# Both feature halves of a token tile projected in one block in every second attention step

## The chip, the cores and the metric

The kernel runs on one core of one Trainium2 chip. The metric is device time in microseconds (us) from the start to the end of the program. The engines are named as in the profile: PE is TensorE (matrix products; PEld are its weight loads), DVE is VectorE, ACT is ScalarE, POOL is GpSimd, and SP is SyncE, which here only issues DMAs. PE writes its results to PSUM, which has eight banks of 512 float32 per partition; DVE and ACT read them there, POOL and the DMAs cannot.

## The reference, cut to what matters

```python
def encoder_layer(x, w_in, rpb, w_fourier, b_fourier, g_pre, g_na, g_f, w_out, g_post):
    h = rms_norm(x, g_pre)
    q, k, v, z_a, u_f, z_f = jnp.split(h @ w_in, [...], axis=-1)     # 512 columns each
    y_a = neighbourhood_attention(q, k, v, rpb)   # 8 heads of 64, window 8 rows x 16 columns
    y_f = fourier_mix(u_f, w_fourier, b_fourier)  # fft2, then @ w_fourier + b_fourier
    mixed = jnp.concatenate([rms_norm(y_a, g_na) * jax.nn.silu(z_a),
                             rms_norm(y_f, g_f) * jax.nn.silu(z_f)], axis=-1)
    out = mixed @ w_out                           # (tokens, 1024) @ (1024, 1024)
    return x + rms_norm(out, g_post)
```

It is applied to a prompt of 256 tokens and to a sample of 2048 tokens (a grid of 32 rows by 64 columns), 2304 tokens together, in float32.

## The kernel before, in words

The kernel works in four stages: the input projections (up to about 554 us), the Fourier part (to about 611 us), a stage of 36 steps that computes the attention and beside it the Fourier half of the output projection (to about 850 us), and the attention half of the output projection with the last norm (to the end). The change lies in the third stage.

**A step.** The attention is cut into 36 groups, `G[0]` to `G[35]`: nine for each of four pairs of heads (`pr, i = divmod(k, 9)`). Group `i == 0` is the prompt (a block of 128 key columns), `i == 1, 2` are the top and bottom rows of the sample, and `i == 3` to `8` are its middle rows, the largest kind. Every group has two blocks of query columns (`b`), one with 32 and one with 24 key columns a row, and two heads (`h`), so four tiles of scores. The loop over `k` from 2 to 37 is a software pipeline. In step `k`

- `transp` turns the finished probabilities of group `k-2` on PE into four banks, `ptb[0]` to `ptb[3]`; ACT and DVE copy two banks each to the tile `pt`;
- `scores` forms the four score tiles of group `k` on PE. Three lie in the three banks of the ring `"a"`, the fourth (`b = 1, h = 1`) in the single bank of the ring `"c"`;
- `bias_max` (DVE, an instruction for each score tile and one that reads its accumulator) adds the bias and takes the row maximum; `exps` (ACT) takes the exponential; `soft` takes the reciprocal of the sums (DVE) and scales the probabilities (POOL, two instructions a block);
- `f_mm` multiplies a tile of 128 tokens of the Fourier half by one half (512 columns) of the output weights: twelve matmuls, since both factors are split in a high and a low part;
- `pv` multiplies the probabilities of group `k-2` by the values. Its result goes to the same single bank `"c"`, and is read there by DVE (`y`, times the gate) and by ACT (`sqa` or `ysq`, the squares).

**The projection beside it.** `ftiles[t]` is a tile of 128 tokens, 18 in all. `ys_load` fetches it, `ys_mul` (POOL) multiplies it by its gate, `ys_split` makes the high part `yh` (ACT) and the low part `yl` (DVE). Step `k` projects one feature half, `k % 2`, of tile `k // 2`. `f_evac` takes the result out of PSUM, scaled by the norm factor `invf`: the first half on DVE, the second on ACT, and a DMA stores the tile `ofs`. `f_norm` (in steps 4, 8, 10, 12) and `a_norm` (32, 34, 36) sum squares on PE and start the computation of norm factors, which `run_later` finishes. `YSQ` squares the last two blocks of the Fourier output in steps 2 to 7.

**What sets the order.** In this stage all five engines run their instructions in the order in which the program writes them; nothing reorders them. An instruction that waits holds up all that stands behind it on its engine. Semaphores between engines follow from the tiles: who reads a bank must have finished before PE writes it again.

The end of a step before, from `f_mm` on:

```python
            f_mm(k)
        ...
        run_later()
        ...
        if k % 2 and x < 18:
            ys_split(ftiles[x])
        ...
        if g:
            f_evac(k)
        pv(f)
```

Of the kernel before, what the change touches and what calls it, by code (L numbers as in the profile page):

```python
# [13 lines left out]
ALU = mybir.AluOpType  # L14
# [165 lines left out]
def build(tc, A, O):  # L180
# [976 lines left out]
    def scores(g):  # L1157
        nr = g["nr"]
        kk = KK[g["pr"]].rearrange("p (r c) -> p r c", c=64)
        if "w" in g:  # L1160
            sp = [ps.tile([128, 352], F32, tag="c", name="s", bufs=1), *ptb,
                  ps.tile([128, 352], F32, tag="a", name="s", bufs=3)]
        else:
            sp = [ps.tile([128, 352], F32, tag="c" if x == 3 else "a", name="s", bufs=1 if x == 3 else 3)
                  for x in range(4)]
        R = g["R"]
        for b, w in enumerate(g["kw"]):
            if R is None:
                seq = [(y, 0, 4, 0, KP0[2 * b + y]) for y in range(2)]
            else:  # L1170
                c0, r = KC0[2 * g["hc"] + b], 4 + HALF[R][0] - 4 * (R > 0)
                seq = [(0, r, 11, 0, c0), (1, r + 12, 3, 0, c0), (1, r + 4, 8, 3, c0)] if R else \
                    [(y, r + 24 * y, 8, 0, c0) for y in range(2)]
            for y, k, n, j, c0 in seq:
                for h in range(2):
                    hs = slice(64 * h, 64 * h + 64)
                    nc.tensor.matmul(sp[2 * b + h][64 * y:64 * y + 64, j * w:(j + n) * w],  # L1177
                                     g["q"][hs, 128 * b + 64 * y:128 * b + 64 * y + 64],
                                     kk[hs, k:k + n, c0:c0 + w], start=True, stop=True)
        g["s"] = sp  # L1180
        if "w" in g:
            return
        wide = [w == 32 and (g["R"] is not None or b) for b, w in enumerate(g["kw"])]
        g["w"] = [jp.tile([128, 2, 352 if x else 264], F32, tag="ww" if x else "wn", name="w", bufs=WB) for x in wide]
        g["m"] = [jp.tile([128, 8], F32, tag="m", name="m", bufs=4) for b in range(2)]
# [4 lines left out]
    def bias_max(g, b, h):  # L1190
        nr, w = g["nr"], g["kw"][b]
        n = nr * w
        if g["R"] is None:
            tv = rows(TB[g["pr"], 0][:, (2 * b + h) * n:(2 * b + h) * n + n], w)
        else:
            x0 = (g["R"] == 0) * 512 + h * nr * 80
            c0 = (0, 24, 24, 56)[2 * g["hc"] + b]
            tv = rows(TB[g["pr"], int(g["R"] > 0)][:, x0:x0 + nr * 80], 80)[:, :, c0:c0 + w]
        nc.vector.tensor_tensor_reduce(out=rows(g["w"][b][:, h, :n], w), in0=rows(g["s"][2 * b + h][:, :n], w), in1=tv,  # L1199
                               scale=1.0, scalar=3.0e38, op0=ALU.add, op1=ALU.min, accum_out=g["m"][b][:, h:h + 1])  # L1200
# [5 lines left out]
    def soft(g, b):  # L1206
        m = g["m"][b]
        nc.vector.reciprocal(m[:, 4:6], m[:, 2:4])  # L1208
        for h in range(2):
            w = g["w"][b][:, h, :g["nr"] * g["kw"][b]]  # L1210
            nc.gpsimd.tensor_scalar(w, w, m[:, 4 + h:5 + h], 1.0, ALU.mult, ALU.mult)  # L1211
# [175 lines left out]
    def ys_load(d):  # L1387
        t, half = d["t"], d["half"]
        ts = slice(t * 128, t * 128 + 128)
        d["raw"] = sm.tile([128, 4, 128], F32, tag="yr", name="yr", bufs=3)  # L1390
        nc.sync.dma_start(d["raw"], yD[half, :, :, ts].rearrange("c p t -> p c t"))
        if half:
            d["z"] = sm.tile([128, 4, 128], F32, tag="yz", name="yz", bufs=1)
            nc.sync.dma_start(d["z"], zD[0, :, ts].rearrange("(c p) t -> p c t", p=128))

    def ys_mul(d):
        if d["half"]:
            nc.gpsimd.tensor_tensor(out=d["raw"], in0=d["raw"], in1=d["z"], op=ALU.mult)
# [19 lines left out]
    def out_mm(d, n, js, p, w):  # L1418
        for j in js:
            c, x = divmod(j, 3)  # L1420
            nc.tensor.matmul(p, (d["l"] if x == 2 else d["h"])[:, c], w(n, int(x == 1), c), start=j == 0, stop=j == 11)  # L1421
# [6 lines left out]
        d["xt"] = gt([128, D], F32, "xt")  # L1428
        nc.sync.dma_start(d["xt"], A["xn"][d["t"] * 128:d["t"] * 128 + 128, :])

    def bank(k):
        return ptb[k if k < 2 else 2 + k % 2]

    def f_mm(k):
        d, n = ftiles[k // 2], k % 2
        d["p"] = bank(k)
        out_mm(d, n, range(12), d["p"], lambda n, x, c: wo1[n][c][:, x])

    def a_mm(d, n):
        x = n or d is atiles[0]  # L1440
# [1 line left out]
        d["p", n] = p  # L1442
        out_mm(d, n, range(12), p, lambda n, x, c: WO[x][:, c, n * 512:n * 512 + 512])

    def f_evac(k):
        d, n = ftiles[k // 2], k % 2
        t, p = d["t"], d.pop("p")
        if n == 0:
            d["o"] = gt([128, D], F32, "ofs")
        o = d["o"]  # L1450
        ns = slice(n * 512, n * 512 + 512)
        if n:
            nc.scalar.activation(o[:, ns], p, AF.Copy, scale=invf[:, t:t + 1])
            nc.sync.dma_start(oD[t * 128:t * 128 + 128, :], o)
        else:
            V.tensor_scalar(o[:, ns], p, invf[:, t:t + 1], None, ALU.mult)  # L1456
# [33 lines left out]
    def pv(g):  # L1490
# [35 lines left out]
        if R is None or hc:  # L1526
# [8 lines left out]

    NT = {4: range(2, 4), 8: range(4, 8), 10: range(8, 13), 12: range(13, 18)}

    YSQ = {2: [(Y2, 256, 512), (Y2, 512, 1024)], 3: [(Y, 256, 512), (Y2, 1024, 1664)], 4: [(Y2, 1664, 2304)],
           5: [(Y, 512, 1110)], 6: [(Y, 1110, 1708)], 7: [(Y, 1708, 2304)]}
    ftiles[0]["h"], ftiles[0]["l"] = y0h  # L1540
    y_parts(ftiles[1])
    ftiles[1]["raw"], ftiles[1]["z"] = y0[:, 0], y0[:, 1]
    nc.sync.dma_start(yD[1, 3, :, TP:], Y[:, TP:])
    f_mm(0)
    f_norm(range(2))
    ys_mul(ftiles[1])
    ptb += [ps.tile([128, 512], F32, tag="b", name="ptb", bufs=2) for x in range(2)]
    for x in range(2, 4):
        V.memset(ptb[x], 0.0)
    run_later()  # L1550
    f_evac(0)
    f_mm(1)
    ys_split(ftiles[1])
    f_evac(1)
    ys_load(ftiles[2])
    prep_v(G[2])
    prep(G[4])
# [1 line left out]
    for k in range(2, len(G) + 2):  # L1559
        pr, i = divmod(k, 9)  # L1560
        g, p, f = G[k] if k < len(G) else None, G[k - 1] if k <= len(G) else None, G[k - 2]
        if pr < 3:
            if i == 3:
                load_k(pr + 1)
            if i == 5:
                load_t(pr + 1, 0)
        if 0 < pr < 4 and i == 0:
            load_t(pr, 1)
        if k == 9:
            nc.sync.dma_start(gpb, pbc(A["gpost"]))  # L1570
        if k == 23:
            wp = pt.enter_context(tc.tile_pool(name="wp", bufs=1, side="right"))
            WO.extend(wp.tile([128, 4, D], F32R, name="w0%d" % x) for x in range(2))
        if 24 <= k < 32:
            y = k - 24
            nc.sync.dma_start(WO[y % 2][:, y // 2].bitcast(F32), woD[0, y % 2, y // 2])
        x = k // 2 + 1
        transp(f)
        if p:
            soft(p, 1)  # L1580
        if g:
            scores(g)
            if k < 34 and k % 2 == 0:
                ys_mul(ftiles[x])
                if x + 1 < 18:
                    ys_load(ftiles[x + 1])
            bias_max(g, 0, 0)
            exps(g, 0, 0)
            bias_max(g, 0, 1)
            exps(g, 0, 1)  # L1590
            bias_max(g, 1, 0)
            exps(g, 1, 0)
            bias_max(g, 1, 1)
            soft(g, 0)
            exps(g, 1, 1)
            f_mm(k)
        else:
            a_mm(atiles[0], k - 36)
        if k in NT:
            f_norm(NT[k])  # L1600
        if k in (32, 34, 36):
            a_norm(atiles[{32: slice(6), 34: slice(6, 10), 36: slice(10, 14)}[k]])
        run_later()
        for v, x0, x1 in YSQ.get(k, []):
            nc.scalar.activation(v[:, x0:x1], v[:, x0:x1], AF.Square)
            V.tensor_tensor(out=sqs[:, x0:x1], in0=sqs[:, x0:x1], in1=v[:, x0:x1], op=ALU.add)
        if pr < 3 and i == 7:
            mask_p(pr + 1)
        if k % 2 and x < 18:
            ys_split(ftiles[x])  # L1610
        if k == 34:
            ys_split(atiles[0])
        if g:
            f_evac(k)
        pv(f)
        if k == 12:
            pq_.close()
        if k + 1 < len(G):
            prep_v(G[k + 1])
        if k + 4 < len(G):  # L1620
            prep(G[k + 4])
        if k == 28:
            xk = [kp.tile([128, T], F32, tag=x, name="xk", bufs=n) for x, n in (("kh", 2), ("kl", 1))]
        if 32 <= k < 36:
            x, d = k - 32, atiles[k - 32]
            d["xt"] = xk[x // 2][:, x % 2 * D:x % 2 * D + D]
            nc.sync.dma_start(d["xt"], A["xn"][d["t"] * 128:d["t"] * 128 + 128, :])
        if k == 32:
            ys_load(atiles[0])
        if k in (34, 35):  # L1630
            ys_load(atiles[k - 33])
            of_load(atiles[k - 34])
        if k == 36:
            ys_split(atiles[1])
# [114 lines left out]
```

## Time and profile before

| | us |
|---|---|
| median of 3 runs (951.89 to 953.03) | 952.01 |
| the profiled execution | 952.14 |
| its span, from the first instruction to the last | 950.3 |
| attention stage, steps 2 to 37, in the trace | about 618 to 848.5 |
| PE busy in the span | 936.1 (99%) |
| DVE busy | 663.7 (70%) |
| ACT busy | 467.3 (49%) |
| POOL busy | 332.5 (35%) |

How to read the rows that follow. A row of the timeline has the start and the length in us, the engine, the line of the kernel, the operation, `out<-in` by the program's names, shapes, a count, and in square brackets the idle time of the engine just before, with what ended it. Several instructions in a row may be merged to one row. A row of the chain (the work that ended last, followed back) has start, length and what it was; "issue" in it is time in which nothing that the profile shows was waited for. A row of stretches has the busy time of each engine, the number of instructions, and, ahead of the DMA share, the granted clock of PE (1.00 is full). DVE's instructions are pipelined: a row's length runs past the next row's start.

### The profile page before, as it was taken

To read this page: it belongs to the slowest core of one execution; us is meant where nothing else is said; L and a number is where in the kernel's file an instruction comes from. 1 tells how busy PE (TensorE), PEld (TensorE's weight loads), DVE (VectorE), ACT (ScalarE), POOL (GpSimd) and SP (SyncE) were. 2 spreads that over 40 slices of the span, in tenths; PEclk is the share of its full clock that TensorE was granted. 3 is DMA by queue.
4 is the path that set the end of the run, shared out by engine and by line. 5 is a ranking of instruction groups with operands and counts; after the bars stand their busy time and mean duration, and the time that the engine had idled before them with its cause. 6 is when DMAs were issued, how large, how long until landed. Compare 5 with 4: busy or idle time off the path is not lost.

```text
span 950.3 us, 18824 instructions
## 1 busy us (share of the span) xinstructions
PE 936.1 (99%) x6800; PEld 780.1 (82%) x6800; DVE 663.7 (70%) x1305; ACT 467.3 (49%) x1035; POOL 332.5 (35%) x338
## 2 busy tenths in 40 slices
PE   9999999999999999999999999989999999999996
PEld 7889988888888888888888897968777777888885
DVE  6387987676875966686767454676565665649997
ACT  6746676532233643233344234566655666544443
POOL 3101202435650400543533000434445565324444
PEclk9999999999999999999999999999999999999999
DMA  9899676468575999669979789688887899959993
GB/s 337 313 371 371 219 284 248 165 226 309 204 284 201 353 410 329 244 229 318 331 260 322 269 307 327 225 248 231 258 256 230 248 301 285 284 195 368 338 341 124
DMA packets 146846, 265.20 MB, mean 279 GB/s; under 512 B 21889, under 2 KB 86785, under 8 KB 143873
## 3 DMA queue, kind: packets, MB, share of 16 engines
q1 hardware_dynamic: 146608, 263.99, 80.4%
q8 instruction: 54, 0.88, 0.4%
q14 instruction: 40, 0.32, 0.1%
q10 hardware_dynamic: 144, 0.00, 0.0%
HBM read 175.40 MB, written 95.88 MB: 285 GB/s over the span
## 4 chain that ended last, share of the span: by engine, by line
PE 93%; DVE 2%; DMA 2%; issue 1%; ACT 1%; SPq 0%; DVEq 0%; ACTq 0%
PE mm L176 18%; PE mm L177 18%; PE mm L175 18%; PE ptb L1421 10%; PE po L1421 10%; PE pv L1498 4%; PE s L1177 4%; PE ptb L1482 3%; PE pab L1015 2%; PE py L175 1%; PE py L177 1%; PE py L176 1%; DMA za<-zD 1%; DVE ofs L1456 0%; DMA rv<-wv 0%
## 5 line engine op out<-in xcount | busy, mean ns | idle before, releaser
L175 PE MATMUL mm<-xh,wa 128*128 128x512 f32 x448 | 174.4, 389 | 0.0
L176 PE MATMUL mm<-xl,wa 128*128 128x512 f32 x448 | 174.3, 389 | 0.0
L177 PE MATMUL mm<-xh,wa 128*128 128x512 f32 x448 | 174.3, 389 | 0.0
L176 PEld LDWEIGHTS mm<-xl,wa 128*128 128x128 f32 x448 | 84.1, 188 | 17.5
L177 PEld LDWEIGHTS mm<-xh,wa 128*128 128x128 f32 x448 | 84.1, 188 | 17.4
L175 PEld LDWEIGHTS mm<-xh,wa 128*128 128x128 f32 x448 | 84.1, 188 | 17.4
L1421 PE MATMUL ptb<-wo,yh 128*128 128x512 f32 x272 | 88.2, 405 | 0.5 <-ACT pt L1485 0.3
L1421 PE MATMUL po<-w,yh 128*128 128x512 f32 x280 | 86.6, 391 | 0.0
L552 POOL TENSOR_TENSOR ws<-wr 128x512 f32<-128x512 f32 x16 | 22.5, 1407 | 183.1 <-DMA wr<-wz 176.2
L1211 POOL TENSOR_SCALAR w<-w,m 128x352 f32<-128x352 f32 (+4 forms) x136 | 65.9, 499 | 46.6 <-DVE m L1208 26.2
L567 DVE TENSOR_TENSOR wa<-wr,wa 128x512 fp32r<-128x512 f32 x60 | 55.9, 938 | 33.2 <-ACT wa L566 33.2
L1204 ACT ACTIVATE w<-w,m 128x352 f32<-128x352 f32 (+4 forms) x136 | 69.7, 515 | 17.0 <-DVE m L1199 16.9
L869 DVE TENSOR_TENSOR f<-u,mm 128x512 f32<-128x512 f32 x64 | 43.5, 680 | 34.1 <-PE mm L177 29.4
L176 PE MATMUL mm<-vl,xh 128*128 128x512 f32 x168 | 65.5, 390 | 0.2 <-DVE vl L498 0.2
L177 PE MATMUL mm<-vh,xl 128*128 128x512 f32 x168 | 65.4, 389 | 0.0
L175 PE MATMUL mm<-vh,xh 128*128 128x512 f32 x168 | 65.4, 389 | 0.0
L1421 PEld LDWEIGHTS ptb<-wo,yh 128*128 128x128 f32 x272 | 48.4, 188 | 20.2 <-ACT pt L1485 5.6
L1421 PEld LDWEIGHTS po<-w,yh 128*128 128x128 f32 x280 | 52.2, 188 | 10.9
L566 ACT CAST wa<-wr 128x512 fp32r<-128x512 f32 x60 | 36.5, 618 | 40.4 <-PE mm L177 22.4
L1421 PE MATMUL po<-w,yl 128*128 128x512 f32 x140 | 54.5, 389 | 0.0
L1498 PEld LDWEIGHTS pv<-pt,v 96*64 96x64 f32 (+2 forms) x1280 | 45.2, 137 | 10.3 <-issue 5.6
L1421 PE MATMUL ptb<-wo,yl 128*128 128x512 f32 x136 | 53.2, 391 | 0.0
(246 smaller groups left out, 2167.8 us busy)
## 6 DMA issues: line engine op xcount, KB each, us to landing
wr<-wz SPq DMA_DIRECT2D x48, 512.0 KB
vl<-sD SPq DMA_DIRECT2D x20, 512.0 KB
xm<-xm SPq DMA_DIRECT2D x9, 1024.0 KB
oD<-ofs SPq DMA_DIRECT2D x18, 512.0 KB
of<-oD SPq DMA_DIRECT2D x18, 512.0 KB
yr<-yD SPq DMA_DIRECT2D x34, 256.0 KB
zD<-f SPq DMA_DIRECT2D x16, 512.0 KB
woD<-wo SPq DMA_DIRECT2D x16, 512.0 KB
```

The costliest lines, as they stand in the source:

```text
L175: nc.tensor.matmul(out, lh, rh, start=first, stop=False)
L176: nc.tensor.matmul(out, lh, rl, start=False, stop=False)
L177: nc.tensor.matmul(out, ll, rh, start=False, stop=last)
L566: nc.scalar.copy(o[:, 0], src)
L567: nc.vector.tensor_tensor(out=o[:, 1], in0=src, in1=o[:, 0].bitcast(F32), op=ALU.subtract)
L869: nc.vector.tensor_tensor(out=dst(f, b), in0=src(uu[u]), in1=src(p), op=op)
L1177: nc.tensor.matmul(sp[2 * b + h][64 * y:64 * y + 64, j * w:(j + n) * w], g["q"][hs, 128 * b + 64 * y:128 * b + 64 * y + 64], kk[hs, k:k + ...
L1204: nc.scalar.activation(w, w, AF.Exp, bias=m[:, h:h + 1], scale=-1.0, accum_out=m[:, 2 + h:3 + h])
L1211: nc.gpsimd.tensor_scalar(w, w, m[:, 4 + h:5 + h], 1.0, ALU.mult, ALU.mult)
L1421: nc.tensor.matmul(p, (d["l"] if x == 2 else d["h"])[:, c], w(n, int(x == 1), c), start=j == 0, stop=j == 11)
L1482: nc.tensor.transpose(ptb[2 * b + y][:nk, x:x + 64], g["w"][b][ys, h, c0:c0 + nk], ident[ys, ys])
L1498: nc.tensor.matmul(p[hs, b, o], v[:nk, b, x, hs], g["pt"][b][:nk, h, j * 128 + o.start:j * 128 + o.stop], start=first, stop=last)
```

## The change

A step is now short or long. An odd step has no projection: PE does `transp`, `scores` and `pv` alone. An even step `k` projects both halves of tile `k // 2`, with `f_mm(..., 0)` and `f_mm(..., 1)` one behind the other (the norm's small products between them where there are any). They go to the banks `ptb[0]` and `ptb[1]`; before, from step 2 on, they went to `ptb[2]` and `ptb[3]`. In an odd step `bias_max` is done for all four tiles, but `exps` only for the first block (`b = 0`). The exponentials of the second block, and both `soft` of an odd group, move to the even step that follows; an even group has both of its `soft` in its own step. `ys_mul`, `ys_load` and `ys_split` of the next tile, the two `f_evac` and the squares of `YSQ` (now in steps 2, 4, 6, 8) all stand in even steps. What is computed, and by how many instructions, stays the same.

```diff
-    def f_mm(k):
-        d, n = ftiles[k // 2], k % 2
-        d["p"] = bank(k)
-        out_mm(d, n, range(12), d["p"], lambda n, x, c: wo1[n][c][:, x])
+    def f_mm(d, n):
+        d["p", n] = ptb[n]
+        out_mm(d, n, range(12), ptb[n], lambda n, x, c: wo1[n][c][:, x])
...
-    YSQ = {2: [(Y2, 256, 512), (Y2, 512, 1024)], 3: [(Y, 256, 512), (Y2, 1024, 1664)], 4: [(Y2, 1664, 2304)],
-           5: [(Y, 512, 1110)], 6: [(Y, 1110, 1708)], 7: [(Y, 1708, 2304)]}
+    YSQ = {2: [(Y2, 256, 512), (Y, 256, 512), (Y2, 512, 1024)], 4: [(Y2, 1024, 1664), (Y, 512, 1110)],
+           6: [(Y2, 1664, 2304), (Y, 1110, 1708)], 8: [(Y, 1708, 2304)]}
...
         transp(f)
-        if p:
-            soft(p, 1)
-        if g:
-            scores(g)
-            if k < 34 and k % 2 == 0:
-                ys_mul(ftiles[x])
-                if x + 1 < 18:
-                    ys_load(ftiles[x + 1])
-            bias_max(g, 0, 0)
-            exps(g, 0, 0)
-            bias_max(g, 0, 1)
-            exps(g, 0, 1)
-            bias_max(g, 1, 0)
-            exps(g, 1, 0)
-            bias_max(g, 1, 1)
-            soft(g, 0)
-            exps(g, 1, 1)
-            f_mm(k)
+        if k % 2:
+            if g:
+                scores(g)
+                for b in range(2):
+                    for h in range(2):
+                        bias_max(g, b, h)
+                        if b == 0:
+                            exps(g, b, h)
+            else:
+                a_mm(atiles[0], 1)
         else:
-            a_mm(atiles[0], k - 36)
...
+            if k > 2:
+                soft(p, 0)
+                exps(p, 1, 0)
+                exps(p, 1, 1)
+            if g:
+                scores(g)
+                bias_max(g, 0, 0)
+                exps(g, 0, 0)
+                bias_max(g, 0, 1)
+                exps(g, 0, 1)
+                soft(p, 1)
+                for h in range(2):
+                    bias_max(g, 1, h)
+                    exps(g, 1, h)
+                if x < 17:
+                    ys_mul(ftiles[x + 1])
+                if x < 16:
+                    ys_load(ftiles[x + 2])
+                f_mm(ftiles[x], 0)
...
+            if g:
+                f_mm(ftiles[x], 1)
+                soft(g, 0)
+            run_later()
+            if g:
+                f_evac(ftiles[x], 0)
+                soft(g, 1)
+            for v, x0, x1 in YSQ.get(k, []):
+                nc.scalar.activation(v[:, x0:x1], v[:, x0:x1], AF.Square)
+                V.tensor_tensor(out=sqs[:, x0:x1], in0=sqs[:, x0:x1], in1=v[:, x0:x1], op=ALU.add)
+            if x < 17:
+                ys_split(ftiles[x + 1])
...
+            if g:
+                f_evac(ftiles[x], 1)
...
         pv(f)
```

The order of the instructions shows it at step 25 (odd, a large group). PE before, from the last scores of step 25 to the start of its `pv` (`wo` are the output weights, `yh` and `yl` the parts of the token tile):

```order
L1177 MATMUL s<-kk,q 64x352 x2
L1177 MATMUL s<-kk,q 64x96 x2
L1177 MATMUL s<-kk,q 64x256 x2
L1421 MATMUL ptb<-wo_5155,yh 128x512 x2
L1421 MATMUL ptb<-wo_5155,yl 128x512
L1421 MATMUL ptb<-wo_5156,yh 128x512 x2
L1421 MATMUL ptb<-wo_5156,yl 128x512
L1421 MATMUL ptb<-wo_5157,yh 128x512 x2
L1421 MATMUL ptb<-wo_5157,yl 128x512
L1421 MATMUL ptb<-wo_5158,yh 128x512 x2
L1421 MATMUL ptb<-wo_5158,yl 128x512
L1498 MATMUL pv<-pt,v 64x128 x2
```

PE in the same step now:

```order
L1177 MATMUL s<-kk,q 64x264 x2
L1177 MATMUL s<-kk,q 64x72 x2
L1177 MATMUL s<-kk,q 64x192 x2
L1177 MATMUL s<-kk,q 64x352 x2
L1177 MATMUL s<-kk,q 64x96 x2
L1177 MATMUL s<-kk,q 64x256 x2
L1493 MATMUL pv<-pt,v 64x128 x2
L1493 MATMUL pv<-pt,v 64x64 x8
L1493 MATMUL pv<-pt,v 64x128 x2
L1493 MATMUL pv<-pt,v 64x64 x8
```

The twelve matmuls of the projection that stood between `scores` and `pv` are gone from here; they stand in step 24, behind those of the other half.

DVE before, in step 25 (the row `ISA w,m<-s,tb` is `bias_max`, `ISA m` its accumulator read):

```order
L1518 TENSOR_TENSOR y<-pv,za 128x2x8x16
L1485 COPY pt<-ptb 96x6x64
L1485 COPY pt<-ptb 128x6x64
L1208 RECIPROCAL m<-m 128x2
L1199 ISA w,m<-s,tb 128x264
L1199 ISA m 128x1
L1199 ISA w,m<-s,tb 128x264
L1199 ISA m 128x1
L1199 ISA w,m<-s,tb 128x352
L1199 ISA m 128x1
L1199 ISA w,m<-s,tb 128x352
L1199 ISA m 128x1
```

DVE in the same step now:

```order
L1513 TENSOR_TENSOR y<-pv,za 128x2x8x16
L1480 COPY pt<-ptb 96x6x64
L1480 COPY pt<-ptb 128x6x64
L1199 ISA w,m<-s,tb 128x264
L1199 ISA m 128x1
L1199 ISA w,m<-s,tb 128x264
L1199 ISA m 128x1
L1199 ISA w,m<-s,tb 128x352
L1199 ISA m 128x1
L1199 ISA w,m<-s,tb 128x352
L1199 ISA m 128x1
L1513 TENSOR_TENSOR y<-pv,za 128x2x8x16
```

One reciprocal left the front of the step; behind the last `bias_max`, where a reciprocal and `yl` stood before, the next step's `y` follows at once.

ACT before, in steps 25 and 26 (`w,m<-w,m` is `exps`):

```order
L1524 ACTIVATE sqa<-pv 128x256
L1485 COPY pt<-ptb 96x6x64
L1485 COPY pt<-ptb 128x6x64
L1204 ACTIVATE w,m<-w,m 128x264 x2
L1204 ACTIVATE w,m<-w,m 128x352 x2
L1407 CAST yh<-yr 128x512
L1453 ACTIVATE ofs<-ptb,invf 128x512
L1524 ACTIVATE sqa<-pv 128x256
L1485 COPY pt<-ptb 128x6x64
L1485 COPY pt<-ptb 96x6x64
L1204 ACTIVATE w,m<-w,m 128x352 x2
L1204 ACTIVATE w,m<-w,m 128x264 x2
```

ACT in the same two steps now:

```order
L1519 ACTIVATE sqa<-pv 128x256
L1480 COPY pt<-ptb 96x6x64
L1480 COPY pt<-ptb 128x6x64
L1204 ACTIVATE w,m<-w,m 128x264 x2
L1519 ACTIVATE sqa<-pv 128x256
L1480 COPY pt<-ptb 128x6x64
L1480 COPY pt<-ptb 96x6x64
L1204 ACTIVATE w,m<-w,m 128x352 x4
L1204 ACTIVATE w,m<-w,m 128x264 x2
L1407 CAST yh<-yr 128x512
L1448 ACTIVATE ofs<-ptb,invf 128x512
```

Two of the four exponentials of step 25 went to step 26, where six stand in a row, and the cast and the evacuation stand in the even step behind them.

More of the change, by code (lines that the diff above doesn't have):

```diff
@@ L1429, in xt_load @@
         nc.sync.dma_start(d["xt"], A["xn"][d["t"] * 128:d["t"] * 128 + 128, :])
-    def bank(k):
-        return ptb[k if k < 2 else 2 + k % 2]
-    def f_mm(k):
-        d, n = ftiles[k // 2], k % 2
-        d["p"] = bank(k)
-        out_mm(d, n, range(12), d["p"], lambda n, x, c: wo1[n][c][:, x])
+    def f_mm(d, n):
+        d["p", n] = ptb[n]
+        out_mm(d, n, range(12), ptb[n], lambda n, x, c: wo1[n][c][:, x])
     def a_mm(d, n):
@@ L1443, in a_mm, with f_evac @@
         out_mm(d, n, range(12), p, lambda n, x, c: WO[x][:, c, n * 512:n * 512 + 512])
-    def f_evac(k):
-        d, n = ftiles[k // 2], k % 2
-        t, p = d["t"], d.pop("p")
+    def f_evac(d, n):
+        t, p = d["t"], d.pop(("p", n))
         if n == 0:
@@ L1543, in build @@
     nc.sync.dma_start(yD[1, 3, :, TP:], Y[:, TP:])
-    f_mm(0)
+    f_mm(ftiles[0], 0)
     f_norm(range(2))
@@ L1550, in build @@
     run_later()
-    f_evac(0)
-    f_mm(1)
+    f_evac(ftiles[0], 0)
+    f_mm(ftiles[0], 1)
     ys_split(ftiles[1])
-    f_evac(1)
+    f_evac(ftiles[0], 1)
     ys_load(ftiles[2])
@@ L1576, in build @@
             nc.sync.dma_start(WO[y % 2][:, y // 2].bitcast(F32), woD[0, y % 2, y // 2])
-        x = k // 2 + 1
+        x = k // 2
         transp(f)
-        if p:
-            soft(p, 1)
-        if g:
-            scores(g)
-            if k < 34 and k % 2 == 0:
-                ys_mul(ftiles[x])
-                if x + 1 < 18:
-                    ys_load(ftiles[x + 1])
-            bias_max(g, 0, 0)
-            exps(g, 0, 0)
-            bias_max(g, 0, 1)
-            exps(g, 0, 1)
-            bias_max(g, 1, 0)
-            exps(g, 1, 0)
-            bias_max(g, 1, 1)
-            soft(g, 0)
-            exps(g, 1, 1)
-            f_mm(k)
-        else:
-            a_mm(atiles[0], k - 36)
@@ L1599, in build @@
[L1599 to L1606, printed above, removed]
+        if k % 2:
[8 more added lines that the diff above has]
+                a_mm(atiles[0], 1)
+        else:
+            if k > 2:
[17 more added lines that the diff above has]
+                f_mm(ftiles[x], 0)
+            else:
+                soft(p, 1)
+                a_mm(atiles[0], 0)
+            if k in NT:
+                f_norm(NT[k])
+            if k in (32, 34, 36):
+                a_norm(atiles[{32: slice(6), 34: slice(6, 10), 36: slice(10, 14)}[k]])
+            if g:
[10 more added lines that the diff above has]
+                ys_split(ftiles[x + 1])
+            elif x == 17:
+                ys_split(atiles[0])
+            if g:
+                f_evac(ftiles[x], 1)
@@ L1607, in build @@
         if pr < 3 and i == 7:
             mask_p(pr + 1)
[L1609 to L1614, printed above, removed]
         pv(f)
```

## The prediction

> **What bounds the kernel now.** I read the page first, then the stretch of the attention stage, then the chain inside one step, then the engines beside it.
>
> ```profile
> PE 936.1 (99%) x6800; PEld 780.1 (82%) x6800; DVE 663.7 (70%) x1305; ACT 467.3 (49%) x1035; POOL 332.5 (35%) x338
> 611.00:850.00 239.00, 234.81 (x3284) 188.33 (x3283) 147.15 (x546) 142.00 (x452) 113.15 (x193) 1.00 0.84 252
> 753.00:789.00 36.00, 35.81 (x540) 28.69 (x535) 22.86 (x83) 23.00 (x72) 20.11 (x33) 1.00 0.96 291
> ```
>
> PE is busy all the time. In the stage that changes it idles 239.00 - 234.81 = 4.2 us, and 0.2 of 36.00 us in its steady part. The others are busy for 70% of the span or less. As the change keeps every matmul, 4.2 us is nearly all that better order can win; what it can lose is open. The chain of step 25 (a large group) shows where the time goes:
>
> ```profile
> 764.29 1.52 PE pv L1498 x40
> 765.81 0.83 PE ptb L1482 x23
> 766.64 1.21 PE s L1177 x20
> 767.84 2.94 PE ptb L1421 x12
> 770.79 1.22 PE pv L1498 x29
> ```
>
> Transposes 0.83, scores 1.21, projection 2.94, `pv` 1.52: 6.50 us, nothing but PE. So the question is not how busy the others are but whether PE, at each of its four pieces, finds its banks free. DVE in the same step:
>
> ```profile
> 765.85 0.42 DVE L1518 TENSOR_TENSOR y<-pv,za 128x256 f32<-128x256 f32 x1 [0.78 <-PE pv L1498]
> 766.35 1.02 DVE L1485 COPY pt<-ptb 96x384 f32<-96x384 f32 x2
> 767.28 0.15 DVE L1208 RECIPROCAL m<-m 128x2 f32<-128x2 f32 x1
> 767.43 0.43 DVE L1199 CUSTOM_DVE_ANT_1 w<-s,tb 128x264 f32<-128x264 f32 x1
> ...
> 768.59 0.52 DVE L1199 CUSTOM_DVE_ANT_1 w<-s,tb 128x352 f32<-128x352 f32 x1
> ```
>
> DVE can start only when the last `pv` has ended, at 765.81: `y` frees the bank `"c"`, then come the two copies, then four `bias_max`, the last of which reads bank `"c"` and ends at 768.59 + 0.52 = 769.11. Only then may this step's `pv` write that bank. In the kernel before it starts at 770.79, so 1.68 us of slack are left. The cover is the projection, 2.94 us.
>
> **The change, part by part.** *Odd steps lose their projection (17 steps, 3 to 35).* `pv` would be ready to start where the first matmul of the projection starts now, and must wait for the last `bias_max`. DVE's work ahead of it (`y`, copies, four `bias_max`) stays in the odd step; only ACT's and POOL's work, and reciprocals, leave it. The hole in step 25 is therefore 769.11 less the start of the projection. The odd steps are of four kinds, by the block order and size of their group. Here are the last `bias_max` and the projection's start in steps 25, 31, 29 and 27:
>
> ```profile
> 767.77 0.73 PE L1421 MATMUL ptb<-wo,yh 128*128 128x512 f32 x2
> 768.35 0.39 PE L1421 MATMUL ptb<-wo,yl 128*128 128x512 f32 x1
> 803.75 0.53 DVE L1199 CUSTOM_DVE_ANT_1 w<-s,tb 128x352 f32<-128x352 f32 x1 [0.27 <-PE s L1177]
> 805.00 0.43 DVE L1199 CUSTOM_DVE_ANT_1 w<-s,tb 128x264 f32<-128x264 f32 x1
> 803.95 0.73 PE L1421 MATMUL ptb<-wo,yh 128*128 128x512 f32 x2
> 793.34 0.35 DVE L1199 CUSTOM_DVE_ANT_1 w<-s,tb 128x192 f32<-128x192 f32 x1
> 792.62 0.73 PE L1421 MATMUL ptb<-wo,yh 128*128 128x512 f32 x2
> 780.99 0.28 DVE L1199 CUSTOM_DVE_ANT_0 w<-s,tb 128x128 f32<-128x128 f32 x1
> 780.44 0.73 PE L1421 MATMUL ptb<-wo,yh 128*128 128x512 f32 x2 [0.18 <-DVE pt L1485]
> ```
>
> Narrow block first (3, 5, 7, 21, 23, 25): 769.11 - 767.77 = 1.34, six times, 8.0. Wide block first (13, 15, 17, 31, 33, 35): 805.43 - 803.95 = 1.48, six times, 8.9. Groups at the sample's edge (11, 19, 29): 793.69 - 792.62 = 1.07, three times, 3.2. Prompt (9, 27): 781.27 - 780.44 = 0.83, twice, 1.7. Together 21.8. The trace of before does not show PE waiting for a `bias_max`, so what a release costs is bounded by two others: copies to the projection, and `ofs` to a transpose.
>
> ```profile
> 666.73 0.04 issue
> 666.78 3.04 PE ptb L1421 x12
> ...
> 638.19 0.14 issue
> 638.33 0.57 PE ptb L1482 x12
> ```
>
> 0.04 or 0.14. `pv` begins with small float32 weights as the transposes do, so I take 0.14: 17 x 0.14 = 2.4 (low end 0.7). The reciprocal that leaves DVE's front is worth little: in the first kind `bias_max` started at 767.43 and could not start before the copies end, 766.35 + 1.02 = 767.37, so 6 x 0.06 = 0.4; in the others it waits for scores or copies anyway (0.27 at 803.75). Holes: 21.8 + 2.4 - 0.4 = +23.8.
>
> *PE's waits of before go.* Inside the stage they are these, with the two that lie ahead of step 2's transposes, which the change doesn't touch:
>
> ```profile
> PE ptb L1482 <- DVE ofs L1456: 3.3, 6, 1.3
> PE ptb L1482 <- ACT ofs L1453: 0.4, 1, 0.4
> PE ptb L1421 <- ACT pt L1485: 0.3, 1, 0.3
> 617.94 0.24 PE L1482 MATMUL ptb<-ident,sc 64*128 64x64 f32 x1 [0.17 <-DVE ofs L1456]
> 618.55 0.46 PE L1482 MATMUL ptb<-ident,sc 64*128 64x64 f32 x7 [0.37 <-ACT ofs L1453]
> ```
>
> 3.3 + 0.4 + 0.3 - 0.17 - 0.37 = 3.5. They come from evacuations that are late for the next transposes. In a long step the first evacuation has the second half's 2.94 and `pv`'s 1.52 ahead of those, so I let them go: -3.5 (high end 0). The second, on ACT, is late next: it has only `pv`'s 1.52 to end in, and needs 0.69 behind the cast `yh`'s 0.61:
>
> ```profile
> 770.07 0.61 ACT L1407 CAST yh<-yr 128x512 fp32r<-128x512 f32 x1
> 770.82 0.69 ACT L1453 ACTIVATE ofs<-ptb,invf 128x512 f32<-128x512 f32 x1
> ```
>
> In steps 2, 4, 6 and 8 the squares stand in front of both on ACT, of 256 to 640 elements each where the evacuation has 512. I take nothing for it, and for the high end one square as long as an evacuation in each of the four, +2.8.
>
> *Two blocks joined.* Matmuls inside the block follow each other every 0.23; the first two take 768.35 - 767.77 = 0.58, so 0.12 is lost on entry, and on leaving:
>
> ```profile
> 770.40 0.39 PE L1421 MATMUL ptb<-wo,yl 128*128 128x512 f32 x1
> 770.72 1.59 PE L1498 MATMUL pv<-pt,v 96*64 96x128 f32 x40
> ```
>
> 0.32, 0.09 too much. 0.21 saved a pair, in the eleven long steps without norm products between the halves: -2.2 (0 to 17 x 0.21 = -3.6).
>
> *Moved at no cost.* ACT's and POOL's work of a pair of steps fits into the 9.4 us (0.83 + 1.21 + 2 x 2.94 + 1.52) of the long one: the steady row above gives ACT 23.00 and POOL 20.11 in 36.00, so 8.3 and 7.3 for two steps of 6.50, of which ACT's copies, squares and two exponentials and POOL's additions stay in the odd step. DVE's share is 8.3, of which 769.11 - 765.85 = 3.3 stays odd. If that cover went, the price is rival C's. SP: the store of `ofs` still waits for ACT's evacuation with the loads of the step queued behind it, now once in a long step as before once in an odd one, and PE has no wait of that kind in the list above. `ys_load` now follows a later `ys_mul`, but its tile is used a whole pair (13 us) on; keys, values and gates are asked for one to four steps ahead, and steps get longer. POOL's queue has `soft` of the odd group ahead of `ys_mul`, and `yh` behind that; at 7.3 of 9.4 it holds.
>
> Sum: +23.8 - 3.5 - 2.2 = +18.1. Against the profiled 952.14 that is 970.2; the median of 952.01 stands 0.13 below it, so 970.1. The term ends: low 952.0 + 22.1 - 3.5 - 3.6 = 967.0, high 952.0 + 23.8 + 2.8 = 978.6.
>
> **Rivals.**
>
> *A, faster: DVE's front shrinks.* POOL's scalings leave the odd steps, and POOL can slow DVE: `yl` took 0.69 alone and 1.42 beside POOL.
>
> ```profile
> 757.68 0.69 DVE L1412 TENSOR_TENSOR yl<-yr,yh 128x512 fp32r<-128x512 f32 x1 [1.49 <-ACT yh L1407]
> 770.71 1.42 DVE L1412 TENSOR_TENSOR yl<-yr,yh 128x512 fp32r<-128x512 f32 x1 [1.49 <-ACT yh L1407]
> 770.29 1.28 POOL L1090 TENSOR_TENSOR tb<-cm,tb 128x512 f32<-128x512 f32 x1
> 651.63 1.02 DVE L1485 COPY pt<-ptb 96x384 f32<-96x384 f32 x2
> ```
>
> If the holes closed, only the gains would be left: 952.1 - 3.5 - 2.2 = 946.4. It decides below 5.7 / 17 = 0.34 us a hole, so DVE's 3.3 would have to lose 1.0. Against it: the copies took 1.02 at 651.63 too, between two pieces of POOL's work, and `bias_max` is as long in all steps. 0.06.
>
> *B, the clock falls.* PE would now stop for over a microsecond in every pair. If that halved its clock for the odd step's own work (0.83 + 1.21 + 1.52 = 3.56), 17 x 3.56 = 61 comes on top: 1031. The trace has a stretch of the kind, with 1.29 us of idle time:
>
> ```profile
> 636.00:645.00 9.00, 7.71 (x136) 6.22 (x134) 6.90 (x21) 5.72 (x16) 1.90 (x4) 1.00 1.01 294
> ```
>
> The granted clock stayed 1.00. 0.03. (The Trainium skill, "TensorE: Matmul & The Clock Gate", section on psum-queue depth-cycling, speaks for this rival: a kernel that goes round PSUM banks leaves PE idle for short times between groups of matmuls, often enough that its clock swings between half and full. By that rule the time is the 1031 above, by the row 970.1; the row shows one stop, not seventeen, so it doesn't refute the page.)
>
> *C, the long step has a hole too.* `yh` waits on ACT for POOL's `ys_mul`; the evacuation behind it then ends late for the transposes of the odd step. Cast 0.61 and evacuation 0.69 less the slack 1.52 - 0.69 = 0.83 makes 0.47 a pair; 17 x 0.47 = 8: 978. For it: POOL's work stands in the long step almost whole. Against: about 2 us are free there. 0.11.
>
> **How the numbers follow.** The main case has 0.80; its own range is 966 to 975. Forecast 970.1. The range of 8 in 10 takes in the high end with C, and below the low end room for holes that are a third smaller (970.1 - 24 / 3 = 962): 962 to 978. About 0.2% (2 us) is what a measurement of this kernel can tell. Faster 0.04 (most of A), same 0.02 (A in half), slower 0.94.
>
> **What would show it.** In odd steps an idle time of PE ahead of `pv`, put down to DVE's `w` of line 1199, of 1.2 to 1.6 us in twelve steps and about 1 in five, 24 in all; none ahead of transposes; long large steps of about 9.3 us; the clock at 1.00. I am wrong if `pv` starts right behind the scores, if the holes are shorter because DVE starts ahead of the end of `pv`, or if PE waits in long steps.

## The result and the profile after

| | before | after |
|---|---|---|
| median (lowest to highest), us | 952.32 (951.89 to 953.03), 4 runs | 969.22 (968.30 to 970.37), 4 runs |
| ratio | 1 | 1.0177, 95% interval 1.016 to 1.0195 |
| profiled execution, span | 952.14, 950.3 | 970.12, 968.3 |
| first transpose of step 2 to that of step 37 | 843.14 - 617.94 = 225.2 | 861.21 - 620.29 = 240.9 |

The kernel became 16.9 us slower; 970.1 had been forecast. The stage grew by 15.7. What follows it took as long as before (950.3 - 843.14 = 107.2 and 968.3 - 861.21 = 107.1). In the profiled execution the stage also began 2.35 us later, but that start moves between executions: in the kernels below, which differ only behind it, the first transpose comes between 617.26 and 621.64.

First the page's row of engines and the stretch of the attention stage, then what PE waited for (engine, line, releaser: us in all, times, longest):

```profile
PE 934.7 (97%) x6800; PEld 781.0 (81%) x6800; DVE 665.1 (69%) x1305; ACT 466.6 (48%) x1035; POOL 342.1 (35%) x338
617.00:867.00 250.00, 227.16 (x3259) 184.51 (x3259) 146.43 (x533) 139.05 (x441) 120.35 (x187) 1.00 0.78 239
PE pv L1493 <- ACT w L1204: 13.3, 10, 1.6
PE pv L1493 <- DVE m L1199: 8.9, 7, 1.4
PE ptb L1477 <- DVE ofs L1451: 0.4, 1, 0.4
```

PE has the same 6800 matmuls and is busy as long; it idles 250.00 - 227.16 = 22.8 us in the stage, where it was 4.2. Of that, 13.3 + 8.9 = 22.2 stand in front of `pv`, 17 times, once in each odd step with a group. The waits in front of transposes went, but for the one at the stage's start. Clock 1.00. The chain through steps 25 and 26, without its shortest pieces:

```profile
766.21 0.51 PE ptb L1477 x11
...
767.28 0.53 DVE pt L1480
...
768.52 0.44 DVE w L1199
768.97 0.44 DVE w L1199
769.42 0.14 issue
769.56 1.59 PE pv L1493 x40
771.15 0.84 PE ptb L1477 x23
771.99 1.21 PE s L1177 x20
773.20 5.67 PE ptb L1421 x24
778.87 1.52 PE pv L1493 x40
780.39 0.51 PE ptb L1477 x11
```

The odd step has left PE: its chain runs through DVE's copies and `bias_max`, and 0.14 later `pv` starts. Step 25 takes 771.15 - 766.21 = 4.94, where 6.50 less the projection's 2.94 would be 3.56. Step 26 takes 780.39 - 771.15 = 9.24, all PE. The pair takes 14.18 where it took 13.02.

### The profile page after: what moved, and what is told of

It is laid out like the page before. It is cut to its first block, busy times and chain, and to the rows that moved or that the text cites. A ratio compares the mean times of both kernels' runs of the same rounds, so it can differ in the third digit from the quotient of the medians.

```text
span 968.3 us, 18814 instructions
## 1 busy us (share of the span) xinstructions
PE 934.7 (97%) x6800; PEld 781.0 (81%) x6800; DVE 665.1 (69%) x1305; ACT 466.6 (48%) x1035; POOL 342.1 (35%) x338
## 4 chain that ended last, share of the span: by engine, by line
PE 87%; DVE 3%; DMA 3%; ACT 3%; issue 2%; SPq 1%; POOL 0%; DVEq 0%; ACTq 0%; POOLq 0%
PE mm L177 16%; PE mm L176 16%; PE mm L175 16%; PE po L1421 10%; PE ptb L1421 10%; PE pv L1493 5%; PE s L1177 3%; PE ptb L1477 2%; PE pab L1015 2%; DMA xr<-xt 1%; DMA xm<-xm 1%; ACT xm L309 1%; ACT w L1204 1%; DVE w L1199 1%; PE py L175 1%
## 5 line engine op out<-in xcount | busy, mean ns | idle before, releaser
L1211 POOL TENSOR_SCALAR w<-w,m 128x352 f32<-128x352 f32 (+4 forms) x136 | 75.0, 565 | 40.0 <-DVE m L1208 21.9
L1493 PE MATMUL pv<-pt,v 96*64 96x64 f32 (+4 forms) x1280 | 50.2, 231 | 22.2 <-ACT w L1204 13.3
L1513 DVE TENSOR_TENSOR y<-pv,za 128x256 f32<-128x256 f32 (+1 forms) x40 | 15.5, 396 | 58.0 <-PE pv L1493 58.0
```

What stands on the lines that cost most here:

```text
L1493: nc.tensor.matmul(p[hs, b, o], v[:nk, b, x, hs], g["pt"][b][:nk, h, j * 128 + o.start:j * 128 + o.stop], start=first, stop=last)
```

## The experiments

The rivals for the 17 us were: the exponentials and scalings moved to the long steps; ACT as the one that releases `pv`, which the profile names in ten of the seventeen holes; and PE's own pace. The theory is the prediction's: `pv` shares one PSUM bank with the fourth score tile, and its last reader, `bias_max`, is done 1.3 us too late once no projection stands in between.

**The projection alone moved.** Exponentials, reciprocals and scalings stand where they stood before:

```diff
 odd:   +  soft(p, 1); scores(g)
        +  bias_max and exps of all four tiles, soft(g, 0) ahead of the last exps
 even:  -  soft(p, 0), exps(p, 1, 0), exps(p, 1, 1), soft(g, 0), soft(g, 1)
        +  soft(p, 1) at the start, all four exps and soft(g, 0) as before
```

> The projection alone stands in the long steps as in the changed kernel; exponentials, reciprocals and scalings stand where they stood before the change. Theory: DVE's front in the odd steps has one reciprocal more, which costs at most 0.06 in six of them; the holes stay 22 to 23 us: 969.2 to 970. Rival 1 (moved exponentials and scalings cost the time): 952. Rival 2 (ACT releases pv): the four exponentials end 0.8 us later than the two did, the holes grow by about 14: 983.

Measured: 969.43 (968.63 to 970.03), ratio to the kernel before 1.0173 (1.0159 to 1.0187). In front of `pv` PE waited 13.4 + 6.7 + 2.5 = 22.6 us. The moved exponentials and scalings cost nothing and gain nothing; the whole loss comes with the projection and with what moved along with it (evacuation, product with the gate, split, squares). ACT's rival fails here too: four exponentials instead of two should have given 983.

**No exponentials in odd steps.**

```diff
 odd:   -  exps(g, 0, h) behind bias_max(g, 0, h)
 even:  +  exps(p, 0, 0); exps(p, 0, 1)   # ahead of soft(p, 0)
```

> As the changed kernel, but odd steps hold no exponentials at all: the first block's two move to the next long step as well, ahead of the second block's. ACT then ends in an odd step with its two copies, over a microsecond ahead of the last bias_max. Theory (DVE's last bias_max releases pv, although the trace names ACT's exponentials in ten holes): all seventeen holes stay as long, 22 us, and the trace names DVE for every one: 969. Rival (ACT's exponentials release pv in the ten): those ten shrink or go, 13 us less: 956.

Measured: 969.19 (968.77 to 971.55), ratio 1.018 (1.0165 to 1.0195). PE's waits of this kernel, and step 17's hole, which was 1.46 and put down to ACT in the changed kernel:

```profile
PE pv L1493 <- DVE m L1199: 16.1, 12, 1.6
PE pv L1493 <- issue: 6.1, 5, 1.4
730.44 1.59 PE L1493 MATMUL pv<-pt,v 128*64 128x128 f32 x40 [1.46 <-DVE m L1199]
```

16.1 + 6.1 = 22.2, as before, and ACT is named no more. So ACT released nothing: its exponentials had only ended when `pv` started (730.56 and 730.57 in step 17 of the changed kernel, where the last `bias_max` had ended at 730.42, 0.15 earlier). For five holes the profile names nobody, where DVE was expected for all.

**Work for the holes.** Five matmuls that nobody needs are put into each:

```diff
 odd, behind bias_max:
+  for j in range(5):
+      nc.tensor.matmul(ptb[2], ftiles[x]["h"][:, 0], wo1[0][0][:, 0], start=j == 0, stop=j == 4)
```

> The changed kernel with five more matmuls (128x512, of the projection's kind, into a bank that is free there, their result unused) between the scores and pv of each of the seventeen odd steps: 85 matmuls, about 1.35 us a step on PE, 23 us in all. Theory (PE stands there waiting for the last bias_max, so work put there is free until the hole is full): the twelve large holes of about 1.4 take it whole, the five of about 1.0 to 1.3 overflow by up to 0.3: 969 to 971. Rival (PE's own pace sets the odd steps, by its clock or by switching between kinds of matmul): 992.

Measured: 969.47 (967.79 to 970.01), ratio 1.0174 (1.0157 to 1.0191). PE in step 25 of this kernel:

```profile
765.90 1.28 PE L1177 MATMUL s<-kk,q 64*64 64x264 f32 x24
767.11 1.43 PE L1583 MATMUL ptb<-wo,yh 128*128 128x512 f32 x5
768.47 1.59 PE L1493 MATMUL pv<-pt,v 96*64 96x128 f32 x40
```

`pv` follows at once, with no wait, and the step is as long (4.92, was 4.94): 85 matmuls at no cost. PE's pace or clock isn't what costs.

**The shared bank read first.** `bias_max` of odd steps begins with the tile of the shared bank, first with PE's order left alone, then with the second block's scores computed first:

```diff
-  scores(g)
-  bias_max in the order (0,0) (0,1) (1,0) (1,1)
+  scores(g)                  # first run; second run: scores(g, (1, 0))
+  bias_max in the order (1,1) (0,0) (0,1) (1,0)   # second run: (1,1) (1,0) (0,0) (0,1)
```

> As the changed kernel, but in odd steps bias_max takes the tile of the shared bank first, while PE's order of the scores stays: that tile is the last to be computed. Theory: its bias_max starts about 0.15 us after PE's scores, takes 0.52 (wide) or 0.43, and 0.15 to release: holes of 0.82 and 0.73 in the large steps, about 0.5 in the five others, 11.8 in all instead of 22.2: 958.8. Rival 1 (moved exponentials): 969. Rival 2 (ACT): 970 or more, as the exponentials of the first block start 0.4 to 0.5 later.

> Odd steps compute the second block's scores first, and bias_max starts with the tile in the bank that pv needs; nothing else differs from the changed kernel. Theory (pv waits in odd steps for the last bias_max, because the fourth score tile and pv share one bank): the first tile is ready 0.8 to 0.9 us after the scores start, its bias_max takes 0.43 or 0.52, the release 0.15, against 1.21 of scores on PE, so a hole of 0.25 to 0.36 is left in the twelve large steps and about 0.2 in the other five: 4.7 us instead of 22.2, so 951.7. Rival 1 (the exponentials and scalings moved into the long steps cost the time): no change, 969. Rival 2 (pv waits for ACT's exponentials, which the trace names in ten of the seventeen holes): those ten holes grow, since the exponentials end later: 970 or more.

Measured: 957.93 (957.20 to 958.26), ratio 1.0052 (1.0036 to 1.0067), and 954.22 (953.58 to 955.65), ratio 1.0014 (1.0005 to 1.0023). PE's waits in front of `pv` in the first:

```profile
PE pv L1493 <- DVE m L1199: 8.4, 12, 0.8
PE pv L1493 <- issue: 3.0, 5, 0.7
```

8.4 + 3.0 = 11.4 against 11.8 expected. The second was expected 2.5 lower. Its trace names only 3.1 of waits in front of `pv`, less than the 4.7 expected, but two other things cost time: a wait of 1.22 that the changed kernel doesn't have, in step 3, and longer scores. From the first score to `pv` the odd steps took 14.3 us less than in the changed kernel, where the named waits shrank by 22.2 - 3.1 = 19.1; so the scores themselves took some 5 us more. In step 25 they took 1.45 instead of 1.28: the tile of the shared bank now comes first, and ACT's square reads that bank until 771.89, 0.13 after the scores start. These rows are the second run's:

```profile
628.04 0.68 PE L1478 MATMUL ptb<-ident,sc 64*96 64x64 f32 x15 [1.22 <-ACT ofs L1449]
771.76 1.45 PE L1178 MATMUL s<-kk,q 64*64 64x352 f32 x24
773.53 0.67 PE L1494 MATMUL pv<-pt,v 96*64 96x128 f32 x12 [0.32 <-DVE m L1200]
```

**Another bank for `pv`.** Here no engine's order changes:

```diff
 pv, odd steps:
-  p = ps.tile([128, 2, 128], F32, tag="c", name="pv", bufs=1)
+  p = ptb[3][:, :256].rearrange("p (b x) -> p b x", b=2)
```

> The changed kernel, with pv of the seventeen odd steps written to the fourth transpose bank, which is free there once DVE has copied it, instead of the bank it shares with the fourth score tile. No order on any engine changes. Theory (the shared bank makes the hole): pv no longer waits for bias_max and starts right behind the scores; the holes (22.2, and 1 more of drained pipeline) go. The price is a new wait in the next long step: its transposes need that bank 0.42 us after they start, and y and the squares read it until 0.88, so 0.45 in seventeen steps, 7.6: 969.2 - 23.2 + 7.6 = 953.6. Rival (DVE's queue as such, whatever the bank, or ACT, holds pv): 969 or more.

Measured: 958.61 (956.84 to 959.12), ratio 1.0054 (1.0037 to 1.007). PE's waits:

```profile
PE ptb L1477 <- ACT sqa L1522: 6.5, 13, 0.8
PE ptb L1477 <- ACT ysq L1518: 1.6, 4, 0.5
```

None in front of `pv`: the holes are gone with the bank alone. The new wait, 6.5 + 1.6 = 8.1 in seventeen steps, was sized 7.6, but the named idle time is not its whole price: in step 26 the transposes took 1.47 from their start to the first score where they took 0.84. In the even steps together they took 12.6 us longer, while the odd steps gave back 22.5 from the first score to `pv` (23.2 expected). So the new wait cost 12.6 and not 7.6, and that is where the 5 us above the forecast lie.

**The narrow block first, with the shared bank.** The tile of the shared bank always belongs to the narrow block:

```diff
+  c = int(g["kw"][0] >= g["kw"][1])
+  scores(g, (c, 1 - c), 2 * c + 1)        # the last argument: which tile gets the bank "c"
+  bias_max in the order (c,1) (c,0) (1-c,0) (1-c,1)
```

> As the run that begins with the tile of the shared bank, but that tile is always one of the narrow block, which is scored and reduced first. Theory (the hole is the time to the first tile, its bias_max and the release, less the scores): the six odd steps that had the wide block first lose 0.33 instead of 0.57 us each, 1.4 in all; the others stay: 954.2 - 1.4 = 952.8, level with the kernel before. If the order of the blocks doesn't matter: 954.

Measured: 953.62 (952.06 to 956.84), ratio 0.9999 (0.999 to 1.0009): level with the kernel before. Step 25 took 3.88 (4.12 in the run that scores the second block first), so the pair of steps 24 and 25 took 13.11 against 13.02. No version beat the kernel before.

**Half of the projection back in the odd step.** Two runs: the second half with its evacuation goes back, and in the second run the splitting of the next tile too.

```diff
 odd:   +  f_mm(ftiles[x], 1)             # behind bias_max
        +  ys_split(ftiles[x + 1])        # second run only
        +  f_evac(ftiles[x], 1)
 even:  -  f_mm(ftiles[x], 1), f_evac(ftiles[x], 1); second run: ys_split
```

> The second half of the projection and its evacuation go back to the odd step; the exponentials, scalings, squares and the splitting of the next tile stay where the change put them. Theory: the cover is back, the holes (22.2) go, the joined blocks' 2.3 come back, and the waits of the kernel before (3.5) stay away, since those came from where the squares and evacuations stood: 969.2 - 22.2 + 2.3 = 949.3, so 3 below the kernel before. Rival 1 (moved exponentials and scalings cost the time): 965 or more. If the waits of before come back: 952 to 953.

> As the run with the second half back in the odd step, and the splitting of the next tile goes back to the odd step too; exponentials and scalings stay where the change put them. Theory (that run's loss came from the split in a step without the second block's cover: POOL's scalings, the product with the gate, ACT's cast, DVE's subtraction end late, DVE's next y behind them frees the shared bank late): the waits of transposes and scores go, and with them most of the 3.5 of the kernel before: 2 to 3 below the kernel before, 950.5. Rival (the exponentials and scalings of an odd group in the next step are the load that such a step can't carry): as that run, 963 to 967.

Measured: 967.09 (963.48 to 967.68), ratio 1.0141 (1.0123 to 1.0159), and 959.82 (956.11 to 963.77), ratio 1.0078 (1.0057 to 1.01). The holes went, and both forecasts missed, by 18 and 9. In steps 22 and 23 of the first, in order: POOL's product with the gate, ACT's cast, DVE's subtraction, DVE's `y`, ACT's square of the same bank, and PE's scores with the last bank late (1.92 in place of 1.28):

```profile
760.70 1.28 POOL L1398 TENSOR_TENSOR yr<-yr,yz 128x512 f32<-128x512 f32 x1
762.02 0.62 ACT L1407 CAST yh<-yr 128x512 fp32r<-128x512 f32 x1 [0.62 <-POOL yr L1398]
762.67 0.92 DVE L1412 TENSOR_TENSOR yl<-yr,yh 128x512 fp32r<-128x512 f32 x1 [0.34 <-ACT yh L1407]
763.52 0.41 DVE L1513 TENSOR_TENSOR y<-pv,za 128x256 f32<-128x256 f32 x1
763.96 0.38 ACT L1519 ACTIVATE sqa<-pv 128x256 f32<-128x256 f32 x1 [1.32 <-DVE y L1513]
763.30 1.92 PE L1177 MATMUL s<-kk,q 64*64 64x264 f32 x24
```

The split depends on POOL, which has the odd group's scalings first. In an even step without the second half (5.86 us here, 6.5 in others) it ends too late, and DVE's `y`, which has nothing to do with it, waits behind it. In a long step the same queue ends in time. With the split moved back the waits of the transposes stay, 5.1 us in eight times. Six of them (4.5 us) follow steps with norm products, two (0.6) follow steps with a short `pv`. By the program's order they are the first half's evacuation, late and in a bank that the very next transposes need first; the profile names the reciprocal `m`, which DVE does right behind that evacuation. The second run's rows:

```profile
PE ptb L1477 <- DVE m L1208: 5.1, 8, 1.2
PE s L1177 <- ACT ysq L1515: 2.0, 2, 1.6
```

The named waits are not all of the loss here either. In the profiled execution of the first run (963.48) the scores of the odd steps took 9.8 us longer than in the kernel before, of which the trace names 4.3. In the second they took 4.5 longer, nearly all of it in steps 3, 5 and 7, which follow steps with squares; in steps 11, 19, 21 and 23, where they had taken 0.5 to 0.6 longer in the first run, they were as fast as before. So the split was the cost that the second expectation named; what remained are the waits of the transposes and the delays of steps 3, 5 and 7. Why the first run's median lies 3.6 above its profiled execution, and why executions of these two kernels spread over 4 to 8 us, stays open.

**The evacuation ahead of squares and split, in the kernel before.**

```diff
         run_later()
+        if g:
+            f_evac(k)
         for v, x0, x1 in YSQ.get(k, []):
...
-        if g:
-            f_evac(k)
         pv(f)
```

> The kernel before, with one edit: the evacuation of the projection stands ahead of the squares and of the splitting instead of behind them. Tests the term of the sum for the waits of before alone: of the 3.5, those of steps 3, 5 and 35 (0.61 + 1.28 + 0.56) come from an evacuation queued behind squares and splits and should go for the most part, those behind the norm's products stay: 2.0 below the kernel before. If such waits only move to another bank: no change.

Measured: 961.37 (959.89 to 961.64), ratio 1.0087 (1.0075 to 1.01): 9 slower, where 2 faster was expected. DVE and PE in step 3:

```profile
623.10 1.76 DVE L1608 TENSOR_TENSOR sqs<-sqs,Y 128x512 f32<-128x512 f32 x1
624.78 0.47 DVE L1518 TENSOR_TENSOR y<-pv,za 128x128 f32<-128x128 f32 x2
625.85 0.82 PE L1177 MATMUL s<-kk,q 64*64 64x352 f32 x10 [1.21 <-ACT ysq L1520]
```

The evacuation waits for the projection's end, and now the squares' additions and the split wait behind it; DVE's `y` comes behind those, so the shared bank is late for the scores. A wait of 0.61 in front of the transposes became one of 1.21 in the scores. Over the stage the scores took 10.8 us longer and the transposes 2.3 less.

## Why the prediction was right

- **What bounds.** PE did the same work in the same busy time; only its idle time changed, from 4.2 to 22.8 us in the stage. Right.
- **The hole.** Forecast 23.8 us in seventeen steps, 1.42 to 1.62 in the large ones; measured 22.2 of idle time, 1.19 to 1.56 in the large ones. The first, one of the middle, step 25 with the scores ahead of it, and the last:

```profile
632.04 1.15 PE L1493 MATMUL pv<-pt,v 96*64 96x64 f32 x32 [1.19 <-DVE m L1199]
730.57 1.59 PE L1493 MATMUL pv<-pt,v 128*64 128x128 f32 x40 [1.46 <-ACT w L1204]
766.97 1.28 PE L1177 MATMUL s<-kk,q 64*64 64x264 f32 x24
769.56 1.59 PE L1493 MATMUL pv<-pt,v 96*64 96x128 f32 x40 [1.31 <-DVE m L1199]
853.58 1.59 PE L1493 MATMUL pv<-pt,v 128*64 128x128 f32 x40 [1.56 <-ACT w L1204]
```

 The release was sized right (0.14 in the chain above). The trace counts the idle time from the end of the last scores; the next matmul could start some 0.07 earlier (in step 26 the scores end at 773.20, where the chain above lets the projection begin, but its first matmul starts at 773.13). Counted by starts, from the first score to `pv`, step 25 lost 769.56 - 766.97 - 1.20 = 1.39 (1.20 from the first score to the projection before; forecast 1.42), and the seventeen steps 23.6. Ten holes were put down to ACT, which the forecast did not expect; the run without exponentials showed that ACT was not the cause. The bank as the cause is shown by four runs that leave the projection where the change put it: another bank, two orders of `bias_max`, and free matmuls.
- **DVE's front.** In step 25 it shrank from 3.26 to 769.41 - 766.26 = 3.15, by 0.11 for the reciprocal where 0.06 was allowed:

```profile
766.26 0.42 DVE L1513 TENSOR_TENSOR y<-pv,za 128x256 f32<-128x256 f32 x1 [1.71 <-PE pv L1493]
766.80 1.02 DVE L1480 COPY pt<-ptb 96x384 f32<-96x384 f32 x2
767.74 0.42 DVE L1199 CUSTOM_DVE_ANT_1 w<-s,tb 128x264 f32<-128x264 f32 x1
768.89 0.52 DVE L1199 CUSTOM_DVE_ANT_1 w<-s,tb 128x352 f32<-128x352 f32 x1
```

 Rival A needed 1.0. The copies (1.02) and `bias_max` (0.42 and 0.52) are as long as before, though POOL's scalings, which ran beside `bias_max` before (from 767.63 in step 25), are gone from there.
- **The waits of before** (-3.5) went, as the list shows: only 0.4 is left, at the stage's start. Whether they could be had without the long step is open: the one edit that tried it, the early evacuation, lost 9.
- **The joined blocks.** 5.67 for both against 2 x 2.94: 0.21 a pair, as read from entry and exit. The steps with norm products between the halves, for which nothing was counted, saved a little (step 10: 10.13 against 7.23, so 2.90 more where 2.94 were added). Over all steps the projections with their norm products took 2.9 less; forecast 2.2.
- **The sum.** Counted by starts, step by step: holes +23.6, projections -2.9, and the rest, mostly transposes that no longer wait, -5.0, which makes +15.7, what the stage grew by; forecast +23.8 - 2.2 - 3.5 = +18.1. So the hole was sized right, and the waits of before were undersized by 1.5: the forecast counted the 0.37 of 618.55, which stands among step 2's transposes, as lying ahead of them, and by starts the waits were longer than their idle time (1.50 where the trace names 1.28, in step 5). The joining was undersized by 0.7. The measured medians are 16.9 apart; the 1.2 between lies outside the stage and within what its start moves. That 969.2 came so near to 970.1, with the stage 2.4 off, is in part luck.
- **Rival B.** Seventeen stops of 1.0 to 1.6 us, one in every 14 us, left the granted clock at 1.00. The swing between half and full clock of which the Trainium skill tells ("TensorE: Matmul & The Clock Gate", section on psum-queue depth-cycling) did not come here.
- **Rival C** did not happen in the changed kernel: no transposes wait in the steps. The queue it feared is real, though: with the second half taken out of the long step (above), POOL's product, ACT's cast and DVE's subtraction end late, and it is then DVE's `y` and the scores that pay, where the rival had named ACT's evacuation.

## What to carry to other kernels

Where PE is always busy, ask of every block of matmuls what it hides before moving it: here 2.94 us of projection stood between two users of one PSUM bank whose reader needs 1.3 us beyond the scores, and the slack (1.6 to 1.7) was smaller than the block. The remedy is not where the moved work went but in the order of the bank's reader: reducing that tile first gave back 15 of 17 us. In queues that run in order, a reordering that removes one wait must be followed to whatever stands behind the moved instruction on its engine; twice here a small gain in view turned into a larger wait on a bank that the moved work never touches.

## What the runs showed of the hardware that was not expected

A release named by the profile can be a coincidence: ACT was named for ten holes (13.3 us), and they stayed as long with its work gone. In the kernel with the early evacuation, an addition of 512 columns on DVE took 1.76 while POOL multiplied a token tile by its gate and then scaled probabilities beside it; one of 640 columns took 0.83 there with POOL idle. That POOL is the cause is argued from this overlap and from `yl` in the prediction; no run took POOL's work away.

```profile
631.31 0.83 DVE L1608 TENSOR_TENSOR sqs<-sqs,Y 128x640 f32<-128x640 f32 x1 [0.21 <-ACT Y L1607]
622.91 1.40 POOL L1398 TENSOR_TENSOR yr<-yr,yz 128x512 f32<-128x512 f32 x1 [3.08 <-DMA yz<-zD]
```
